# Attention projected before the convolution in two token groups, mLSTM heads taken up earlier in the weave, and first-key one-hots compared straight into fp32 rows

## The chip, the cores and the metric

The kernel runs on one core of a Trainium2 chip. The metric is the device time of one execution in microseconds (us); the median of three runs before the change is 3003.34 us (2999.98 to 3008.87). Engines are named as in the profile: PE is the tensor engine's matmul (PEld its weight load), DVE the vector engine, ACT the scalar engine, POOL the GpSimd engine, SP the engine that issues most DMAs. An engine takes its instructions in one fixed order; where the first of them waits, all behind it wait.

## The reference, cut to what matters

One decoder layer on 1024 tokens of width 1024. The normalised input is projected to an mLSTM branch (values, an output gate z, input and forget gates, and a branch that goes through a causal convolution over four tokens and a SiLU) and to an attention branch (q, k, v for 8 heads of 64). Both branches are joined, projected and added to x. Then a PEER layer picks, for each token and each of 8 heads, 16 of 16384 experts: each expert is named by a pair of keys out of 128 and 128, and the output is the gated sum of `expert_v` rows weighted by `gelu(h . expert_u)`.

```
c = silu(causal_short_conv(u) + b);  q, k = c @ wq, c @ wk        # mLSTM, per head
h = mlstm_chunkwise(q, k, v, ipre, fpre);  ym = sigmoid(z) * (rms_norm(h) + skip * c)
ya = softmax-combined dilated attention(rms_norm(qa), rms_norm(ka), va)
x = x + concat(ym, ya) @ w_out
idx, gate = top16 over (s1[key1] + s2[key2]);  a = gelu(h2 . expert_u[idx]) * gate
out = x + sum_k a[k] * expert_v[idx[k]]
```

## The kernel before, in words

Tokens are cut into eight tiles of 128 and three groups: group 0 is tiles 0 and 1, group 1 tiles 2 to 5, group 2 tiles 6 and 7. Per group the code issues `channels_in` (normalise, transpose and split the input into two fp32r parts, tiles `hth` and `htl`), `project_values` (accumulators `accvm`, `accz`), `project_gates` (`pif`, then small DVE work and transposes), `project_conv` (`accu`; then on ACT and DVE the four-tap sum `cy`, a sigmoid and a product; result `c` stored to DRAM by SP), `project_attention` (k, q, v in that order, `accqk` and `accva`; k and q normalised, transposed and stored to DRAM by ACT's queue). Every projection goes through `stream`, which loads weights `wr` in three buffers on SP's queue, rounds them on ACT (`wh`, line 170), takes the remainder on DVE (`wl`, line 172) and issues three matmuls for each product. The accumulators have two PSUM banks; for group 1 one stream fills both.

`attention` then runs over head pairs, heads and query tiles: it loads `qp`, `kp`, `vp` and the bias `bt` back from DRAM on SP, and each step computes scores (`sc`, minimum and bias on DVE, line 515, exponential on ACT) and the values of the step before. The mLSTM heads are a second generator: `weave` advances it by one half-head after every `every`-th attention step, that is after the last of each four (of each two in group 2). A half-head loads `cT`, `zs`, `vm` and two weights on SP, and is a chain of small steps over PE, ACT, DVE and POOL that ends in the product `mix` (line 476). `queries` (output projection `acco`, second norm, query projection `accq`, top 16 by DVE) follows. The four tiles of group 1 go to dense experts: their gates are spread by `spread_gates` to a table of tokens by all experts in DRAM (`gate_d`), and `dense_experts` runs all 16384 experts over these 512 tokens on PE, until the end of the program. Tiles 0, 1, 6 and 7 instead gather expert rows by indirect DMA on POOL (line 806, five buffers `gt`): steps U0, U1, V0, V1, U6, V6, U7, V7, with dot products on DVE (line 818, line 863) or, for V0 and V1, matmuls `pov` (line 849).

`spread_gates` works in groups of four tokens: DVE compares the first and the second key of each of the 128 chosen experts with the numbers 0 to 127 (line 727, two bf16 one-hot tiles `hot`), ACT copies the first to fp32 `e1` (line 731), the second is multiplied by the gate into fp32 `e2` (line 735 on ACT, four small instructions, in every other group; line 737 on DVE in the rest), four matmuls `pg` make the table's part (line 742) and ACT copies it out (line 743). There are 4 tiles x 8 blocks x 4 groups = 128 such groups. In the profile both `e1` and `e2` are called `e`.

The code gives the order of priority; a planner with its own costs places the instructions on the engines, and pulls later work (gathers, the next group's projections, queries) into holes. Tiles of a closed scope give their space to later scopes, and a tile that is placed there waits for the last reader of the old one. The scope of `hth` and `htl` is closed after the group's last projection, and for groups 1 and 2 the attention's scope is opened after that on the same side of memory.

Of the kernel before, what the change touches and what calls it, by code (L numbers as in the profile page):

```python
# [15 lines left out]
BF16 = mybir.dt.bfloat16  # L16
AF = mybir.ActivationFunctionType
ALU = mybir.AluOpType
AX = mybir.AxisListType

P = 128
# [22 lines left out]
def hybrid_layer(ctx, tc, x, g1, w_in, w_if, conv_w, conv_b, wq, wk, if_b, mh_g, skip, qn_g, kn_g,  # L44
                 rel_bias, onehot, w_out, g2, w_query, keys, expert_u, expert_ut, expert_v, out, dbg=None):
    nc = tc.nc
# [17 lines left out]
    def pool(name, side="left"):  # L64
        return tc.tile_pool(name=name, bufs=1, side=side, reuse_waits="tile")
# [32 lines left out]
    key128 = consts.tile([P, P, TQ], BF16, name="key128")  # L98
# [55 lines left out]
    def mm3(ps, lh, ll, rh, rl, first, last):  # L154
        nc.tensor.matmul(ps, lh, rh, start=first, stop=False)  # L155
        nc.tensor.matmul(ps, lh, rl, start=False, stop=False)  # L156
        nc.tensor.matmul(ps, ll, rh, start=False, stop=last)  # L157
# [8 lines left out]
    def halves(w_ap):  # L166
        wr = wts.tile([P, 512], F32, name="wr", bufs=3)
        nc.sync.dma_start(wr, w_ap)
        wh = wts.tile([P, 512], F32R, name="wh", bufs=3)
        nc.scalar.copy(wh, wr)  # L170
        wl = wts.tile([P, 512], F32R, name="wl", bufs=3)
        nc.vector.tensor_tensor(wl, wr, wh.bitcast(F32), op=ALU.subtract)  # L172
        return wh, wl
# [68 lines left out]
    def project_gates(g, cl, th, tl):  # L242
        n = GROUPS[g][1]
        W = n * P
        with pool("ga") as ga:
            pif = pst.tile([64, W], F32, name="pif", tag="tp")
            wh, wl = halves(w_if)
            for k in range(KD):
                s = slice(k * 64, (k + 1) * 64)
                mm3(pif, wh[:, s], wl[:, s], th[:, k], tl[:, k], k == 0, k == KD - 1)  # L250
            gi = ga.tile([MH, n, P], F32, name="gi")
            nc.scalar.activation(gi.rearrange("p c t -> p (c t)"), pif[0:MH], AF.Identity, bias=ifb_s[0:MH])
            gf0 = ga.tile([64, W], F32, name="gf0")
            nc.scalar.activation(gf0[32:32 + MH], pif[32:32 + MH], AF.Identity, bias=ifb_s[32:32 + MH])
            gf = ga.tile([MH, W], F32, name="gf")
            nc.vector.tensor_copy(gf, gf0[32:32 + MH])
            return gates(g, cl, ga, gi, gf)

    def project_conv(g, th, tl):

        n = GROUPS[g][1]
        W = n * P
        with pool("su") as st:
            for blk in range(2):
                accs = by_channel(stream(w_in, blk, th, tl, n, True, "u"), n)
                for h, a in enumerate(accs, 2 * blk):
                    uh = st.tile([P, 3 + W], F32, name="uh", bufs=2)
                    nc.vector.tensor_copy(uh[:, 0:3], halo[:, h])
                    nc.scalar.copy(uh[:, 3:], a)
                    nc.vector.tensor_copy(halo[:, h], uh[:, W:W + 3])  # L270
                    y = st.tile([P, W], F32, name="cy", bufs=2)
                    nc.scalar.activation(y, uh[:, 0:W], AF.Identity, scale=cw_s[:, h, 0:1], bias=cb_s[:, h:h + 1])
                    for j in range(1, 4):
                        nc.vector.scalar_tensor_tensor(y, uh[:, j:j + W], cw_s[:, h, j:j + 1], y,
                                                       op0=ALU.mult, op1=ALU.add)
                    nc.scalar.activation(uh[:, 0:W], y, AF.Sigmoid)
                    nc.vector.tensor_tensor(y, y, uh[:, 0:W], op=ALU.mult)
                    c_d[g, h] = dram.tile([P, W], F32, name=f"c{g}{h}")
                    nc.sync.dma_start(c_d[g, h], y)
# [15 lines left out]
    def by_channel(banks, n):  # L295
        return [banks[i * n // 4][:, (i * n * P) % 512:(i * n * P) % 512 + n * P] for i in range(2)]
# [11 lines left out]
    def project_attention(g, th, tl):  # L308

        tile0, n = GROUPS[g]  # L310
        with pool("sb") as st:
            for blk0, dst, gn, nm in ((8, kT_d, kg_s, "k"), (6, qT_d, qg_s, "q")):
                for blk in range(2):
                    qs = st.tile([P, n, 4, AD], F32, name="qs")
                    for b, a in enumerate(stream(w_in, blk0 + blk, th, tl, n, False, "qk")):
                        q = qs[:, 2 * b:2 * b + 2].rearrange("p c h d -> p (c h) d")
                        nc.scalar.copy(q, a.rearrange("p (h d) -> p h d", d=AD))
                        sq = st.tile([P, 8, AD], F32, name="sq")
                        nc.scalar.activation(sq, q, AF.Square)
                        ss = st.tile([P, 8], F32, name="ssq", bufs=2)  # L320
                        nc.vector.tensor_reduce(ss, sq, AX.X, ALU.add)
                        r = rstd(ss, AD, 8, st, "rq")
                        nc.vector.tensor_tensor(q, q, r[:, :, None].to_broadcast([P, 8, AD]), op=ALU.mult)
                    for pl in range(2):
                        pr = 2 * blk + pl
                        pt = pst.tile([P, n * P], F32, name="ptq", tag="tp")
                        for i in range(n):
                            nc.tensor.transpose(pt[:, i * P:(i + 1) * P], qs[:, i, 2 * pl:2 * pl + 2], ident)
                        ev = st.tile([P, n * P], F32, name="ev", bufs=2)
                        nc.scalar.activation(ev, pt, AF.Copy, scale=gn[:, pr:pr + 1])  # L330
                        dst[g, pr] = dram.tile([P, n * P], F32, name=f"{nm}T{g}{pr}")
                        nc.scalar.dma_start(dst[g, pr], ev)
            token_blocks(g, st, 10, va_d, "va", th, tl)
# [381 lines left out]
    def spread_gates(t, gb, psg):  # L715

        half = TQ
        for b in range(P // TB):
            gs = gb.tile([P, P, TB], F32, name="gs", bufs=2)
            for q in range(TB // half):  # L720
                c0 = b * TB + q * half
                ids, gate = ROWS[t]
                full = [P, P, half]
                hot = []
                for side in range(2):
                    o = gb.tile(full, BF16, name="hot", bufs=6)
                    nc.vector.tensor_tensor(o, ids[:, side, None, c0:c0 + half].to_broadcast(full),
                                            key128, op=ALU.is_equal)
                    hot.append(o.rearrange("p e t -> p t e"))
                e1 = gb.tile([P, half, P], F32, name="e1", bufs=3)  # L730
                nc.scalar.copy(e1, hot[0])
                e2 = gb.tile([P, half, P], F32, name="e2", bufs=3)
                if q % 2:
                    for j in range(half):
                        nc.scalar.activation(e2[:, j], hot[1][:, j], AF.Copy, scale=gate[:, c0 + j:c0 + j + 1])  # L735
                else:
                    nc.vector.tensor_tensor(e2, hot[1], gate[:, c0:c0 + half, None].to_broadcast([P, half, P]),
                                            op=ALU.mult)
                for j0 in range(0, half, 4):
                    pg = psg.tile([P, 4, P], F32, name="pg")  # L740
                    for j in range(4):
                        nc.tensor.matmul(pg[:, j], e1[:, j0 + j], e2[:, j0 + j], start=True, stop=True)  # L742
                    nc.scalar.copy(gs[:, :, q * half + j0:q * half + j0 + 4].rearrange("p e t -> p t e"), pg)  # L743
            nc.scalar.dma_start(gate_d[(t - GROUPS[DENSE][0]) * (P // TB) + b], gs.rearrange("p e t -> p (e t)"))
# [125 lines left out]
    def weave(main, other, every):  # L870

        for n, _ in enumerate(main):
            if n % every == every - 1:
                next(other, None)
        return other

# [5 lines left out]
    hx = channels_in(0, hs.tiles)  # L882
# [9 lines left out]
    hx = channels_in(1, hs.tiles)  # L892
# [4 lines left out]
    pt_.close()  # L897
    project_values(1, *hx)
    cols = project_gates(1, cm.tiles, *hx)
    project_conv(1, *hx)  # L900
    project_attention(1, *hx)
    hs.close()
    hs = Scope("hs2", "right")
    mx = Scope("mx1", "right")
# [7 lines left out]
    hx = channels_in(2, hs.tiles)  # L912
    project_values(2, *hx)
    cols = project_gates(2, cm.tiles, *hx)
    project_conv(2, *hx)
    project_attention(2, *hx)
    hs.close()
    drain(queries(1, ql.tiles, "left", cl.tiles, mix))
    ql2 = Scope("ql2")
# [12 lines left out]
    gb = Scope("gb", "right")  # L932
# [18 lines left out]
    for step in "U0 U1 V0 V1 U6 V6 U7 V7".split():  # L951
        t = int(step[1])
# [81 lines left out]
```

## Time and profile before

| | |
|---|---|
| median of three runs | 3003.34 us |
| profiled execution | 3002.0 us |
| its span, first to last instruction | 3000.2 us |
| mean granted TensorE clock | 0.948 of full speed |
| PE busy | 2728.0 us (91%) |
| DVE busy | 2337.4 us (78%) |
| ACT busy | 1237.2 us (41%) |
| POOL busy | 1347.6 us (45%) |
| DMA | 891.50 MB, mean 297 GB/s |

Busy time is the time in which an engine had at least one instruction under way; matmuls overlap, so a busy PE need not be at its peak. The profiled execution is 1.3 us below the median. By the trace the stages follow each other like this: group 0 to about 330 us, the projections of group 1 to about 525 us, attention and mLSTM of group 1 with projections of group 2 to about 850 us, the output and query projections of group 1 with the attention of group 2 to about 1196 us, the spread with the queries of group 2 to about 1534 us, dense experts to the end.

### The profile page before, as it was taken

Reading aid. Unit: us, or ns where it says so; the run is one execution under the profiler, and the core shown is the slowest. Engines: PE = TensorE matmul, PEld = TensorE weight load, DVE = VectorE, ACT = ScalarE, POOL = GpSimd, SP = SyncE. Lnnn points to the kernel's source line nnn. Section 1 sums busy time; section 2 is a strip of 40 time slices with the busy share of each in tenths; the row PEclk is TensorE's granted clock in tenths of the full one; section 3 lists DMA queues with packets and bytes.
Section 4 is the critical chain, followed back from the end, with each engine's and each line's share of the span. In section 5 each row is a group of like instructions: output and inputs, shape, how many; then the busy total and the mean of one; then the engine's idle time right before and its main releaser. Section 6 shows DMA issues by size and latency. Waiting matters only on the chain.

```text
span 3000.2 us, 42795 instructions
## 1 busy us (share of the span) xinstructions
PE 2728.0 (91%) x14382; PEld 2154.0 (72%) x14382; DVE 2337.4 (78%) x5522; ACT 1237.2 (41%) x2311; POOL 1347.6 (45%) x1075
## 2 busy tenths in 40 slices
PE   6978857788989999889899999999999999999999
PEld 5868657476766665567666787777788877788877
DVE  4559897678977889679843789888899888899883
ACT  4643423355534225999952233222233222233222
POOL 0100477435744445423344555555555555556540
PEclk9979978688988999999999999999999999999999
DMA  6644689788998988989898999999999999999992
GB/s 196 188 149 124 241 311 333 267 304 289 342 339 293 310 313 303 327 313 329 306 326 293 325 341 324 327 330 320 316 339 359 329 333 323 329 335 331 336 313 81
DMA packets 370897, 891.50 MB, mean 297 GB/s; under 512 B 34119, under 2 KB 135495, under 8 KB 366580
## 3 DMA queue, kind: packets, MB, share of 16 engines
q0 software_dynamic: 147456, 536.94, 50.5%
q1 hardware_dynamic: 209076, 307.78, 30.8%
q10 hardware_dynamic: 14144, 44.05, 3.8%
q8 instruction: 113, 1.85, 0.2%
q14 instruction: 108, 0.88, 0.1%
HBM read 831.97 MB, written 61.38 MB: 298 GB/s over the span
## 4 chain that ended last, share of the span: by engine, by line
PE 22%; issue 12%; POOL 8%; DMA 7%; DVE 4%; ACT 4%; POOLq 0%; DVEq 0%; ACTq 0%
POOL gt L806 8%; DMA gg<-gate_d 5%; PE pv L156 3%; PE pv L157 3%; PE pu L156 3%; PE pu L155 3%; PE pu L157 3%; PE pv L155 3%; PE pg L742 2%; ACT gs L743 1%; ACT e L735 1%; PE pov L849 1%; DMA gt<-in_expert_u_dram,idx 1%; DVE acc L863 1%; PE accq L194 1%
## 5 line engine op out<-in xcount | busy, mean ns | idle before, releaser
L806 POOL DMA_INDIRECT gt<-in_expert_u_dram,idx x512 | 661.5, 1292 | 646.7 <-DVE gt L818 428.2
L818 DVE SCALAR_TENSOR_TENSOR gt<-gt,h2s 128x1024 f32<-128x1024 f32 x512 | 617.7, 1218 | 65.5 <-DMA gt<-in_expert_u_dram,idx 64.5
L806 POOL DMA_INDIRECT gt<-in_expert_v_dram,idx x256 | 342.3, 1337 | 298.8 <-DVE acc L863 255.2
L806 POOL DMA_INDIRECT gt<-in_expert_v_dram,idxt x256 | 285.9, 1117 | 412.1 <-PE pov L849 359.5
L156 PE MATMUL pv<-vlo,dah 128*128 128x512 f32 x1024 | 402.4, 393 | 9.3 <-DVE vlo L795 9.2
L155 PE MATMUL pu<-h2th,uhi 128*128 128x512 f32 x1024 | 406.4, 397 | 0.5 <-ACT uhi L761 0.4
L156 PE MATMUL pu<-h2tl,uhi 128*128 128x512 f32 x1024 | 405.7, 396 | 0.0
L157 PE MATMUL pu<-h2th,ulo 128*128 128x512 f32 x1024 | 405.6, 396 | 0.0
L157 PE MATMUL pv<-vhi,dal 128*128 128x512 f32 x1024 | 400.4, 391 | 0.0
L793 ACT CAST vhi<-vr 128x512 fp32r<-128x512 f32 x256 | 157.5, 621 | 466.0 <-PE pv L157 459.4
L863 DVE SCALAR_TENSOR_TENSOR acc<-gt,act,acc 128x1024 f32<-128x1024 f32 x256 | 327.6, 1280 | 14.0 <-DMA gt<-in_expert_v_dram,idx 11.7
L155 PE MATMUL pv<-vhi,dah 128*128 128x512 f32 x1024 | 318.7, 394 | 8.3 <-ACT vhi L793 8.3
L170 ACT CAST wh<-wr 128x512 fp32r<-128x512 f32 x291 | 178.8, 620 | 244.9 <-DMA wr<-in_w_in_dram 50.6
L172 DVE TENSOR_TENSOR wl<-wr,wh 128x512 fp32r<-128x512 f32 x291 | 197.7, 684 | 75.4 <-ACT wh L170 72.1
L795 DVE TENSOR_TENSOR vlo<-vr,vhi 128x512 fp32r<-128x512 f32 x256 | 175.3, 686 | 89.3 <-ACT vhi L793 89.1
L156 PEld LDWEIGHTS pv<-vlo,dah 128*128 128x128 f32 x1024 | 193.0, 188 | 60.9 <-DVE vlo L795 14.9
L155 PEld LDWEIGHTS pv<-vhi,dah 128*128 128x128 f32 x1024 | 192.1, 189 | 55.9 <-ACT vhi L793 12.8
L155 PEld LDWEIGHTS pu<-h2th,uhi 128*128 128x128 f32 x1024 | 192.6, 188 | 49.8 <-ACT uhi L761 2.3
L157 PEld LDWEIGHTS pu<-h2th,ulo 128*128 128x128 f32 x1024 | 192.6, 188 | 49.8 <-issue 3.4
L156 PEld LDWEIGHTS pu<-h2tl,uhi 128*128 128x128 f32 x1024 | 192.8, 188 | 47.9 <-issue 2.5
L157 PEld LDWEIGHTS pv<-vhi,dal 128*128 128x128 f32 x1024 | 192.9, 188 | 44.0 <-issue 2.5
L761 ACT CAST uhi<-ur 128x1024 fp32r<-128x1024 f32 x128 | 134.4, 1050 | 214.9 <-PE pu L156 212.8
(278 smaller groups left out, 5596.8 us busy)
## 6 DMA issues: line engine op xcount, KB each, us to landing
ur<-in_expert_ut_dram SPq DMA_DIRECT2D x128, 512.0 KB, 6.2
vr<-in_expert_v_dram SPq DMA_DIRECT2D x256, 256.0 KB, 5.8
wr<-in_w_in_dram SPq DMA_DIRECT2D x144, 256.0 KB, 3.8
gate_d<-gs ACTq DMA_DIRECT2D x32, 1024.0 KB, 8.5
gg<-gate_d SPq DMA_DIRECT2D x16, 2048.0 KB, 20.5
wr<-in_w_query_dram SPq DMA_DIRECT2D x96, 256.0 KB, 4.7
wr<-in_w_out_dram SPq DMA_DIRECT2D x48, 256.0 KB, 4.8
gt<-in_expert_u_dram,idx POOLq DMA_INDIRECT x512, 7.0
```

The source lines that it names most:

```text
L155: nc.tensor.matmul(ps, lh, rh, start=first, stop=False)
L156: nc.tensor.matmul(ps, lh, rl, start=False, stop=False)
L157: nc.tensor.matmul(ps, ll, rh, start=False, stop=last)
L170: nc.scalar.copy(wh, wr)
L172: nc.vector.tensor_tensor(wl, wr, wh.bitcast(F32), op=ALU.subtract)
L742: nc.tensor.matmul(pg[:, j], e1[:, j0 + j], e2[:, j0 + j], start=True, stop=True)
L761: nc.scalar.copy(uh, ur)
L793: nc.scalar.copy(vh, vr)
L795: nc.vector.tensor_tensor(vl, vr, vh.bitcast(F32), op=ALU.subtract)
L806: nc.gpsimd.indirect_dma_start(out=gt, out_offset=None, in_=table, in_offset=bass.IndirectOffsetOnAxis(ap=idx[:, j:j + 1], axis=0))
L818: nc.vector.scalar_tensor_tensor(gt, gt, 1.0, h2, op0=ALU.mult, op1=ALU.mult, accum_out=pr[:, j:j + 1])
L863: nc.vector.scalar_tensor_tensor(acc, gt, COEF[t][:, j:j + 1], acc, op0=ALU.mult, op1=ALU.add)
```

## The change

Three edits. `spread_gates` compares the first keys directly into the fp32 tile `e1`, with tokens outside and keys inside, so the first `hot` tile and the ACT copy are gone; `hot` has three buffers in place of six. `weave` advances the mLSTM after the first attention step of each stretch of `every`, not after the last. In groups 1 and 2 `project_attention` is issued before `project_conv`; group 0 keeps its order.

```
                 e1 = gb.tile([P, half, P], F32, name="e1", bufs=3)
-                nc.scalar.copy(e1, hot[0])
+                nc.vector.tensor_tensor(e1, ids[:, 0, c0:c0 + half, None].to_broadcast([P, half, P]),
+                                        key128.rearrange("p e t -> p t e"), op=ALU.is_equal)
+                o = gb.tile(full, BF16, name="hot", bufs=3)
+                nc.vector.tensor_tensor(o, ids[:, 1, None, c0:c0 + half].to_broadcast(full), key128,
+                                        op=ALU.is_equal)
+                hot = o.rearrange("p e t -> p t e")
...
         for n, _ in enumerate(main):
-            if n % every == every - 1:
+            if n % every == 0:
                 next(other, None)
...
     cols = project_gates(1, cm.tiles, *hx)
+    project_attention(1, *hx)
     project_conv(1, *hx)
-    project_attention(1, *hx)
...
     cols = project_gates(2, cm.tiles, *hx)
+    project_attention(2, *hx)
     project_conv(2, *hx)
-    project_attention(2, *hx)
```

## Rows read from the trace of the kernel before

**Rows 1.** The page's head: span, and busy time by engine.
```profile
span 3000.2 us, 42795 instructions
PE 2728.0 (91%) x14382; PEld 2154.0 (72%) x14382; DVE 2337.4 (78%) x5522; ACT 1237.2 (41%) x2311; POOL 1347.6 (45%) x1075
```

**Rows 2.** Windows: stretch, length, busy PE PEld DVE ACT POOL, clock, DMA, GB/s.
```profile
419.00:432.00 13.00, 0.00 (x0) 0.00 (x0) 13.00 (x23) 2.34 (x4) 8.44 (x7) 0.62 0.93 326
...
834.00:848.00 14.00, 1.32 (x8) 0.73 (x6) 11.83 (x30) 1.78 (x7) 8.88 (x8) 0.67 1.05 405
...
1196.00:1320.00 124.00, 99.73 (x728) 74.92 (x720) 84.16 (x200) 112.40 (x232) 47.41 (x41) 0.92 0.89 320
1320.00:1500.00 180.00, 157.57 (x1213) 124.86 (x1207) 159.26 (x708) 175.40 (x347) 62.34 (x54) 0.98 0.88 317
1500.00:1534.00 34.00, 29.33 (x166) 19.48 (x165) 24.37 (x51) 26.95 (x43) 20.26 (x13) 0.90 0.88 306
1534.00:2924.00 1390.00, 1372.25 (x5962) 1090.53 (x5961) 1124.99 (x1513) 405.13 (x611) 727.23 (x549) 1.00 0.94 329
2924.00:3000.00 76.00, 69.09 (x302) 56.33 (x300) 27.38 (x40) 17.13 (x27) 0.00 (x0) 0.97 0.24 83
```

**Rows 3.** Longest waits of PE from 400 to 560: total us, times, longest.
```profile
PE accqk L194 <- ACT qs L317: 16.0, 3, 13.3
PE sc L513 <- DMA kp<-kT: 14.8, 1, 14.8
PE sc L513 <- DVE mx L515: 5.5, 1, 5.5
```

**Rows 4.** Timeline, group 1's convolution end: start, us, engine, line, idle before it.
```profile
404.78 0.58 ACT L269 COPY uh<-accu 128x512 f32<-128x512 f32 x1 [2.67 <-PE accu L194]
...
431.54 1.07 ACT L317 COPY qs<-accqk 128x512 f32<-128x512 f32 x2 [3.95 <-DVE cy L277]
```

**Rows 5.** Timeline of PE's last value projection and SP's first attention load.
```profile
524.46 0.28 PE L194 MATMUL accva<-wh,htl 128*128 128x256 f32 x1
...
524.54 0.42 SPq L486 DMA_DIRECT2D qp<-qT  x1
```

**Rows 6.** SP's own waits, 330 to 960.
```profile
SPq L168 <- DVE wl L172: 286.4, 75, 22.4
...
SPq L279 <- DVE cy L277: 11.2, 5, 3.8
```

**Rows 7.** Timeline, last mLSTM half-head of group 1 behind its attention.
```profile
822.98 0.66 PE L547 MATMUL pty<-ident,ya 128*128 128x128 f32 x4 [1.06 <-DVE ya L543]
...
844.10 0.69 PE L472 MATMUL pth<-ident,hn 128*128 128x128 f32 x2 [9.69 <-DVE hn L469]
```

**Rows 8.** Groups by line, 1196 to 1540: count, busy, mean ns, idle before.
```profile
L743 ACT COPY gs<-pg 128x512 f32<-128x512 f32 x128 | 130.5, 1061 | 13.5 <-PE pg L742 13.3
...
L727 DVE TENSOR_TENSOR hot<-ids,key 128x512 bf16<-128x512 bf16 x256 | 101.8, 418 | 32.3 <-ACT e L731 25.3 <-ACT e L735 5.8
L735 ACT ACTIVATE e<-hot,grow 128x128 f32<-128x128 bf16 x256 | 84.8, 414 | 0.0
L731 ACT CAST e<-hot 128x512 f32<-128x512 bf16 x128 | 84.5, 670 | 2.7 <-PE pg L742 2.6
...
L737 DVE TENSOR_TENSOR e<-hot,grow 128x512 f32<-128x512 bf16 x64 | 43.6, 683 | 12.8 <-PE pg L742 12.6
```

**Rows 9.** The convolution's tap line: ns least, median, most; both sizes together.
```profile
L274 DVE SCALAR_TENSOR_TENSOR cy<-uh,cw_s,cy x36: 464/480/750, 52.4 to 733.1; 128x256 f32<-128x256 f32 x24, 128x512 f32<-128x512 f32 x12
```

**Rows 10.** Windows of the gathers' line alone (POOL busy, count).
```profile
327.00:960.00 633.00, 324.92 (x261) 0.84 0.89 312
...
1196.00:1534.00 338.00, 128.82 (x106) 0.95 0.88 317
```

**Rows 11.** Window of the `pov` matmuls inside the dense stage.
```profile
1534.00:1670.00 136.00, 22.37 (x168) 3.30 (x168) 0.68 (x1) 1.00 0.89 308
```

**Rows 12.** Timeline of DVE, the last gathered row's work.
```profile
2923.37 1.27 DVE L863 SCALAR_TENSOR_TENSOR acc<-gt,act,acc 128x1024 f32<-128x1024 f32 x1
```

More of the change, by code (lines that the diff above doesn't have):

```diff
@@ L723, in spread_gates @@
                 full = [P, P, half]
[L724 to L729, printed above, removed]
-                e1 = gb.tile([P, half, P], F32, name="e1", bufs=3)
-                nc.scalar.copy(e1, hot[0])
+                e1 = gb.tile([P, half, P], F32, name="e1", bufs=3)
+                nc.vector.tensor_tensor(e1, ids[:, 0, c0:c0 + half, None].to_broadcast([P, half, P]),
[4 more added lines that the diff above has]
+                hot = o.rearrange("p e t -> p t e")
                 e2 = gb.tile([P, half, P], F32, name="e2", bufs=3)
@@ L734, in spread_gates @@
                     for j in range(half):
-                        nc.scalar.activation(e2[:, j], hot[1][:, j], AF.Copy, scale=gate[:, c0 + j:c0 + j + 1])
+                        nc.scalar.activation(e2[:, j], hot[:, j], AF.Copy, scale=gate[:, c0 + j:c0 + j + 1])
                 else:
-                    nc.vector.tensor_tensor(e2, hot[1], gate[:, c0:c0 + half, None].to_broadcast([P, half, P]),
+                    nc.vector.tensor_tensor(e2, hot, gate[:, c0:c0 + half, None].to_broadcast([P, half, P]),
                                             op=ALU.mult)
```

## The prediction

> **What bounds the kernel now.** I read the page's head, then windows by stage, then waits and timelines where PE is empty. The head has PE busy for 91% of the span and DVE for 78% [rows 1]. The last stage, dense experts from 1534, has PE busy for 1372 of 1390 us and again for 69 of the last 76, in which POOL does nothing [rows 2]; PE sets that stage, and the change doesn't touch its work. What the change can move is how early this stage begins. Before it the limits differ.
>
> In the spread (1196 to 1534, 338 us; the three windows of rows 2) ACT is busy for 112.4 + 175.4 + 27.0 = 314.8 us, 93%, DVE for 84.2 + 159.3 + 24.4 = 267.8 (79%) and PE for 99.7 + 157.6 + 29.3 = 286.6 (85%) [rows 2]. ACT paces it: DVE waits 25.3 us for ACT's copy of `e` and PE's pieces follow [rows 8].
>
> In group 1 PE has three empty places. From 419 to 432 it does nothing [rows 2]: the next k projection needs a PSUM bank which ACT's copy `qs` is to empty, and that copy stands in ACT's order behind the convolution's chain, which runs from the accumulator's copy at 405 to the DVE product that lets `qs` go at 431.5; the longest wait is 13.3 us [rows 3, 4]. At 524.5 the last value projection ends and SP loads `qp` 0.08 us later [rows 5]; scores wait 14.8 us for `kp`, then 5.5 for DVE [rows 3]. From 834 to 848 PE is busy for 1.3 of 14 us at a clock of 0.67 [rows 2]: attention's last transposes are at 823, but the last mLSTM half-head, issued after the last attention step, reaches its own transposes at 844 after a 9.7 us wait for DVE [rows 7], and the output projection needs it.
>
> **The change, part by part.** All sums are against the profiled execution's 3002.0 us (span 3000.2 and 1.8 around it); the median of the runs is 1.3 above it, which is added at the end.
>
> *First keys into fp32.* Gone are 128 ACT copies, 84.5 us busy [rows 8], so ACT has 230.3 us left in the stage. Of the 256 bf16 compares at 418 ns, 128 become compares with an fp32 output and a key operand that strides. The trace has no such compare. Its nearest row is line 737: the same two layouts read, the same 128x512 fp32 written, 683 ns; that is the value taken. Ends: 418 (the bf16 compare) [rows 8] and 750 (the slowest three-operand fp32 instruction of that size) [rows 9]; a lower price than 418 is excluded, since neither elements nor written bytes shrink. At 683 DVE gains 128 x 0.265 = 33.9 us and stands at 301.7, more than ACT's 230.3 and PE's 286.6. So DVE becomes the engine that ends last, and the gain is not the 84.5 us removed. I take it that DVE gets as full as ACT is now, 93%, since its largest waits, 25.3 and 5.8 us for ACT, go with the copy: 301.7 / 0.93 = 324, a gain of 14 us. Packed to 100%: 301.7, gain 36. At DVE's present 79%: 382, a loss of 44. At 750 ns DVE has 310.3 and the stage 334, gain 4. At 418 ns PE is next: 286.6 / 0.93 = 308, gain 30. Three `hot` buffers for one tile per group instead of six for two are the same depth: nothing.
>
> The Trainium skill, page "VectorE: DVE Perf Modes", section "The perf-mode tier table", says that a two-tensor operation runs at double rate only where everything is 16-bit, and at single rate with fp32. It speaks against this change: by it the fp32 output alone costs the compare its double rate, and the sum is the one above; without it the 30 us of the lower end would stand. No row here shows the compare itself.
>
> *Attention before the convolution, group 1.* Its 24 weight loads on SP now come ahead of the convolution's 8 and its 4 `c` stores; SP's queue is paced by the weight buffers' release (286.4 us of waits for `wl`, 75 times), not by the `c` stores (11.2 us) [rows 6], so the order costs nothing there by itself. The 13.3 us hole goes, because `qs` no longer stands behind the convolution's chain [rows 3, 4]. What is late next: `qp` was loaded right behind the last reader of the input tiles [rows 5]. I read that as the wait for their space, which now ends with the convolution's last matmul. Then the 14.8 us for `kp` stay, and attention's first minimum on DVE meets the convolution's last chain, which took 26 us from the accumulator's copy [rows 4]. Most of that chain lies in the wait for `kp`; I give back 5 us, about the wait for DVE there now [rows 3]. Net 8 us. Ends: 28 (the hole goes and the convolution also covers the 14.8) and a loss of 13 (13.3 gained, a chain of 26 us wholly in front of the scores). Group 2's swap lies in attention of group 1, beside which its projections run; nothing, and up to 5 either way.
>
> *mLSTM ahead.* Its waits are added where a half-head now stands earlier: its `cT` load waits for the `c` store, behind it on SP stand `zs`, `vm`, weights and the next `kp`; on PE its first matmul holds the scores behind it. Heads 0 and 1 come from the convolution's first block, so I take no cost. The last half-head of group 1 now has three attention steps behind it, so the 9.7 us of rows 7 and the rest of 834 to 848 (14.0 - 1.3 = 12.7 us empty) lie beside those steps: 13 us. Ends: 0 (DVE, 11.8 of 14 us busy there [rows 2], merely shifts its queue) and 20 (from attention's end, 823, to 844, less what matmuls of the half-head still cost). Groups 0 and 2: nothing taken.
>
> *Given back.* POOL issued 261 gathers in 633 us before 960, one per 2.43 us, and 106 in the spread, one per 3.19 [rows 10]. The 21 us of group 1 and 14 of the spread leave 9 + 4 = 13 gathers to later, which end as `pov` matmuls inside the dense stage, where PE has no room: 42 gathers cost it 22.4 us there, 0.53 each [rows 11]. 7 us.
>
> **Sum:** 3002.0 - 14 - 8 - 13 + 7 = 2974; with 1.3 to the median, 2975. The gathers' last work on DVE is at 2923 [rows 12] and holds its place, as the dense stage starts earlier and has more of them; PE's end near 2972 is still behind it.
>
> **The rivals.**
> 1. The spread does not shorten: DVE's order, filled with the top 16 of group 2 and 159 of 180 us busy from 1320 [rows 2], takes up what ACT gives. 3002 - 21 + 9 x 0.53 = 2986, median 2987. For it: that window. Against: from 1196 DVE has 40 of 124 us free.
> 2. The reorder doesn't do what it says: the planner, which places work by its own costs, puts the convolution or the half-heads where they were. 3002 - 14 + 2 = 2990, median 2991. For it: group 2's projections already lie far from their place in the code. Against: the hole at 419 and the tail at 844 follow the code's order.
> 3. All goes well: spread packed (36), group 1's hole and the `kp` wait both covered (28), tail 13, 28 gathers later x 0.53 = 15 back: 2940, median 2941. For it: DVE's waits for ACT were the larger part of its idle time [rows 8]. Against: space of the input tiles.
> 4. Slower: the longer compare leads DVE's order, and DVE keeps its present 79% fill because its remaining waits (PE's `pg`, weights, gather pairs) stay in the same proportion. The spread takes 382 us, +44; 3002 + 44 - 21 - 2 (four gathers fewer later) = 3023, median 3024. It decides once DVE's fill falls under some 85%, where the stage is 355 and eats group 1's gain. For it: the queue is in order, and DVE is in front of both PE and ACT in each group of four. Against: its biggest named waits are the ones removed.
>
> **How the numbers follow.** Chances: forecast 0.44, rival 1 0.17, rival 2 0.14, rival 3 0.10, rival 4 0.15. What a measurement of this kernel can tell from no change is about 0.3%, 9 us. Faster by more (under 2994): nearly all of the forecast, 0.41, most of rival 1, 0.14, over half of rival 2, 0.08, rival 3 0.10: 0.73. Slower (over 3012): rival 4, 0.14. Within: 0.13. The range leaves out half of rival 3 below and most of rival 4 above: 2944 to 3010. The forecast's own is 2958 to 2990.
>
> **What would show it.** In the changed profile: no 128x512 ACT copy to `e`, and 128 compares of 128x512 fp32 near 683 ns on DVE; from the first to the last `pg` some 324 us, with DVE fuller than ACT. PE's wait for `qs` of 13 us gone, and a wait for `kp` of some 15 us still in front of the first scores, now behind `accu` and not `accva`. The last `pth` of group 1 ahead of attention's last `pty`, and no empty 14 us between. More than 42 gathers' `pov` in the dense stage, whose own length stays. Wrong it would be if the spread stays over 335 us (rivals 1, 4), if a first mLSTM half-head holds PE for its `c` load, or if the gathers end after the dense matmuls.

## The result and the profile after

The changed kernel takes 2975.64 us (median of four runs, 2968.47 to 2979.17) where before stands at 3006.11 (four runs, 2999.98 to 3011.11): 0.9886 of it, 95% interval 0.9863 to 0.9909. The quotient of two medians can differ a little from the ratio given (here it is 0.9899); it lies within the interval here and in all comparisons below. The profiled execution took 2979.17 us, 22.8 less than that of before. The forecast of 2975 came out; several of its terms did not.

The head of the page after, to be read beside [rows 1]:

```profile
span 2977.3 us, 42658 instructions
PE 2728.4 (92%) x14382; PEld 2147.5 (72%) x14382; DVE 2365.6 (79%) x5520; ACT 1180.9 (40%) x2187; POOL 1353.4 (45%) x1075
```

PE's busy time is the same (2728.0 before). What the change bought is 23 us less of empty PE.

The windows of the kernel after, columns as in [rows 2]: the old hole behind the convolution, the mLSTM's tail, the spread in three parts, the dense stage and its end:

```profile
405.00:432.00 27.00, 19.05 (x136) 17.53 (x136) 21.89 (x41) 8.99 (x16) 20.98 (x16) 0.94 0.95 330
800.00:818.00 18.00, 0.88 (x7) 0.72 (x7) 10.93 (x24) 0.96 (x5) 9.92 (x11) 0.56 0.99 363
1174.00:1280.00 106.00, 94.58 (x718) 73.88 (x717) 87.16 (x196) 83.97 (x175) 51.68 (x35) 0.95 0.91 333
1280.00:1460.00 180.00, 157.62 (x1241) 121.59 (x1239) 178.45 (x704) 147.83 (x287) 80.12 (x63) 0.99 0.94 342
1460.00:1475.00 15.00, 12.18 (x73) 8.75 (x74) 14.12 (x33) 10.68 (x17) 13.78 (x5) 1.00 0.77 278
1475.00:2901.00 1426.00, 1398.97 (x6084) 1101.73 (x6083) 1123.55 (x1527) 413.20 (x616) 721.41 (x569) 0.99 0.94 327
2901.00:2977.00 76.00, 69.22 (x303) 56.41 (x301) 40.84 (x53) 17.16 (x27) 10.24 (x7) 0.97 0.42 146
```

Three readings. The hole at 419 is gone. The empty place in front of the last mLSTM transposes is not: it has moved to 800 and is longer, PE busy for 0.88 of 18 us at a clock of 0.56. The spread is DVE's now: 178.45 of 180 us in its middle, where ACT has 147.83.

PE's longest waits from 400 to 560 after, as [rows 3] (who waits, for whom, us in total, times, longest; chosen lines):

```profile
PE sc L513 <- DMA kp<-kT: 8.8, 1, 8.8
PE accva L194 <- ACT ev L305: 7.0, 1, 7.0
PE sc L513 <- DVE mx L515: 5.8, 1, 5.8
PE accqk L194 <- ACT qs L317: 3.0, 2, 1.5
```

`qs` holds PE for 1.5 us at most where it was 13.3, `kp` for 8.8 where it was 14.8, and DVE's first minimum for 5.8 where it was 5.5. The last projection of group 1 ends at 503.5 (524.5 before) and the first scores stand at 512.7 (539.6).

The spread's groups after, from 1174 to 1475, as [rows 8] (chosen lines):

```profile
L742 ACT COPY gs<-pg 128x512 f32<-128x512 f32 x127 | 129.9, 1057 | 34.5 <-PE pg L741 27.6 <-issue 4.8 <-DMA gate_d<-gs 1.5
...
L725 DVE TENSOR_TENSOR e<-ids,key 128x512 f32<-128x512 bf16 x125 | 85.1, 685 | 7.4 <-PE pg L741 5.8 <-PE accq L194 1.4 <-issue 0.2
...
L728 DVE TENSOR_TENSOR hot<-ids,key 128x512 bf16<-128x512 bf16 x125 | 50.9, 419 | 3.0 <-issue 2.2 <-ACT e L734 0.7
```

The new compare takes 685 ns (683 forecast), and the waits of 25.3 and 5.8 us for ACT [rows 8] are gone but for 0.7.

### The profile page after: what moved, and what is told of

The parts are those of the page before. It is cut to its first block, busy times and chain, and to the rows that moved or that the text cites. A ratio compares the mean times of both kernels' runs of the same rounds, so it can differ in the third digit from the quotient of the medians.

```text
span 2977.3 us, 42658 instructions
## 1 busy us (share of the span) xinstructions
PE 2728.4 (92%) x14382; PEld 2147.5 (72%) x14382; DVE 2365.6 (79%) x5520; ACT 1180.9 (40%) x2187; POOL 1353.4 (45%) x1075
## 4 chain that ended last, share of the span: by engine, by line
PE 57%; DMA 16%; DVE 13%; issue 7%; POOL 3%; ACT 2%; SPq 0%; DVEq 0%; ACTq 0%; POOLq 0%
DMA gg<-gate_d 7%; PE pu L156 6%; PE pu L157 6%; PE pu L155 6%; PE pv L156 5%; PE pv L157 5%; PE pv L155 5%; DMA gt<-in_expert_v_dram,idxt 3%; PE accq L194 3%; POOL gt L805 3%; PE acco L194 3%; PE pov L848 2%; PE sc L513 2%; PE po L535 2%; DVE gt L817 2%
## 5 line engine op out<-in xcount | busy, mean ns | idle before, releaser
L805 POOL DMA_INDIRECT gt<-in_expert_u_dram,idx x512 | 650.9, 1271 | 692.3 <-DVE gt L817 441.4
L817 DVE SCALAR_TENSOR_TENSOR gt<-gt,h2s 128x1024 f32<-128x1024 f32 x512 | 618.1, 1219 | 58.0 <-DMA gt<-in_expert_u_dram,idx 55.1
L805 POOL DMA_INDIRECT gt<-in_expert_v_dram,idxt x256 | 308.9, 1207 | 373.6 <-PE pov L848 307.7
L156 PEld LDWEIGHTS pv<-vlo,dah 128*128 128x128 f32 x1024 | 193.4, 189 | 59.0 <-DVE vlo L794 10.6
```

Source lines behind the costliest of these rows:

```text
L805: nc.gpsimd.indirect_dma_start(out=gt, out_offset=None, in_=table, in_offset=bass.IndirectOffsetOnAxis(ap=idx[:, j:j + 1], axis=0))
L817: nc.vector.scalar_tensor_tensor(gt, gt, 1.0, h2, op0=ALU.mult, op1=ALU.mult, accum_out=pr[:, j:j + 1])
```

## The experiments

All ran beside the kernel before on their chip, whose median was 3009.57, 3008.13 and 3006.88 us in the three sets. The table holds what the trace of each gives: the first scores of group 1, the first and last `pg` of the spread (us), and, counted from the windows of the dense stage's matmuls `pu` and `pv`, how many of the 6144 were left at 1700 us and how many PE did from 1700 to 2900. How much earlier than before a kernel reaches a point is called its head start; what it loses of that later it gives back. A trace is one execution; its time lies up to 19 us from the median of its kernel, so a sum over a trace is held against the span of that trace.

| kernel | ratio to before, 95% | first `sc` | first, last `pg` | left at 1700 | done to 2900 | span |
|---|---|---|---|---|---|---|
| before | | 539.6 | 1203.0, 1533.0 | 5490 | 5083 | 3000.2 |
| whole change | 0.9886 (0.9863-0.9909) | 512.7 | 1174.9, 1474.8 | 5369 | 5062 | 2977.3 |
| e1 spread alone | 0.9992 (0.9974-1.0011) | 540.8 | 1213.5, 1514.6 | 5466 | 5070 | 2997.8 |
| e2 order alone | 0.9876 (0.9833-0.9919) | 511.8 | 1158.4, 1487.7 | 5368 | 5056 | 2978.3 |
| e3 weave alone | 1.0051 (1.0029-1.0073) | 540.5 | 1231.8, 1572.9 | 5636 | 5123 | 3025.5 |
| e4 order, weave | 0.9941 (0.9912-0.9971) | 508.6 | 1161.7, 1501.6 | 5391 | 5066 | 2981.4 |
| f1 order, spread | 0.9897 (0.9867-0.9927) | 508.4 | 1169.0, 1472.7 | 5396 | 5075 | 2980.4 |
| f2 order, group 1 | 0.9996 (0.9971-1.0020) | 514.6 | 1159.9, 1481.1 | 5412 | 5031 | 2994.4 |
| f3 order, group 2 | 1.0027 (1.0001-1.0053) | 544.4 | 1217.9, 1547.4 | 5603 | 5093 | 3029.1 |
| f4 all, weave in group 1 only | 0.9923 (0.9895-0.9951) | 512.3 | 1158.3, 1455.0 | 5318 | 5064 | 2965.2 |
| h1 before, no U6 V6 U7 V7 | 0.9893 (0.9867-0.9919) | 537.1 | 1200.7, 1549.5 | 5462 | 5202 | 2966.3 |
| h2 f2, no U6 V6 U7 V7 | 0.9758 (0.9732-0.9785) | 506.9 | 1146.8, 1487.9 | 5260 | 5203 | 2919.7 |
| h3 whole, no U6 V6 U7 V7 | 0.9780 (0.9754-0.9806) | 510.0 | 1163.6, 1460.6 | 5299 | 5201 | 2929.0 |

### The three edits apart: e1 to e4

e1, against before:

```
-                hot = []
-                ...
-                nc.scalar.copy(e1, hot[0])
+                nc.vector.tensor_tensor(e1, ids[:, 0, c0:c0 + half, None].to_broadcast([P, half, P]),
+                                        key128.rearrange("p e t -> p t e"), op=ALU.is_equal)
...
```

> The kernel before with the spread edit alone (first keys compared straight into fp32 rows). My sum: 14 us off the spread, 2 given back as gathers' matmuls in the dense stage, so 12 us under the kernel before, and the group 1 milestones (first scores at 540, last mLSTM transposes at 844) where they were. Rival, from the changed kernel's trace, in which the spread is 30 us shorter: 30 off the spread, but 10 to 20 of it back in the dense stage. Rival that the vector engine's order takes it all up: no change within 9 us.

3006.54 us, 0.9992: nothing, although first to last `pg` fell from 330 to 301 us. The number is that of the last forecast, the spread's 29 us that of the second; none of them lasts to the end.

e2, against before, in groups 1 and 2:

```
+    project_attention(1, *hx)
     project_conv(1, *hx)
-    project_attention(1, *hx)
```

> The kernel before with attention's projection ahead of the convolution in groups 1 and 2, nothing else. My sum: the 13.3 us hole at 419 goes, 5 come back at the first scores, 8 us at the first scores and about 4 in the whole. Rival, from the changed kernel's trace, where the first scores come 27 us earlier: 20 to 27 us at the first scores with this edit alone, and 10 to 20 us in the whole, if nothing behind it takes them back.

2978.08 us, 0.9876: as much as the whole change, and more than either forecast. The first scores come 27.8 us earlier. The last `pth` of group 1 lies 31 us behind the last `pty` (21 before) after a wait of 22.6 us for `hn`, though the weave is the old one.

e3, against before:

```
-            if n % every == every - 1:
+            if n % every == 0:
```

> The kernel before with the mLSTM advanced after the first attention step of each stretch, nothing else. My sum: the last mLSTM transposes of group 1 ahead of attention's last transposes, the empty 13 us at 834 gone, about 10 us under the kernel before. Rival, from the changed kernel's trace, in which the last mLSTM transposes come 43 us behind attention's last ones: the mLSTM is a chain of its own that ends when it ends; the last half-head stays behind attention, the empty place stays and the whole moves by less than 6 us.

3027.88 us, 1.0051: a loss of 18 us against its base. The first matmul of an mLSTM head in group 1 did not come earlier (551.1, before 551.6), the attention stage, from first scores to last `pty`, took 294.6 us instead of 283.8, and the last `pth` came at 857 instead of 844, 22 us behind the last `pty` as it was 21 before. Neither forecast had the loss; the rival had the place of the last half-head.

e4 is e2 and e3 together.

> The kernel before with both reorders, without the spread edit. My sum: 21 us off at the start of the output projection, 16 in the whole. Rival, that the group 1 part is a 27 us gain of the order alone and the mLSTM tail takes a part of it back: output projection's end 25 us earlier as in the changed kernel, 15 to 25 in the whole; and with the spread alone the two add up to the whole change's 30 us, or to more if the dense stage takes both back.

2997.12 us, 0.9941: the weave costs beside the new order too, though the two intervals touch (0.9912 against e2's 0.9919); between e4 and the whole change (0.9886) stands the spread edit alone. So the gain is the order's, the weave is no gain, and the spread's 30 us show in the total only behind the other two, if at all. The last set asks for the order without the weave.

### Which group's order, which weave: f1 to f4

f1 is e1 and e2 together, f2 and f3 are e2 in one group only.

> The order in both groups and the spread edit, the weave as before. If the three edits simply add, this is the order's gain (0.9876 of before) and the spread's (0.9992): 0.987, some 2970 us where before stands at 3009. If the spread pays more where the stage begins earlier, as it did behind order and weave together (0.9886 against 0.9941, 0.55%), this is 0.982, some 2956 us, and faster than the whole change. If the whole change owes its time to the weave after all, this stays at or above 0.9886. The spread stage should last 300 us in either case, and first scores should stand at 512.

2979.15 us, 0.9897. Neither faster than the whole change nor than e2: the three intervals overlap over most of their width. The edits don't add. No version tried beats the whole change measurably.

> The order swapped in group 1 alone. Theory 1, that of the prediction: the gain lies in group 1's own projections (hole at 419 gone, first scores 28 us earlier at 512), and group 2's swap is worth nothing; then at least 22 of the 31 us are here, ratio 0.990 or less. Theory 2: group 2's swap shortens the attention of group 1, beside which its projections run (284 us before, 261 with both swaps); then first scores stand at 512, attention still takes 284, and the ratio is 0.995 or more.

> The order swapped in group 2 alone. Theory 1: first scores at 540 as before and a ratio between 0.997 and 1.003. Theory 2: first scores at 540, attention of group 1 in 261 us instead of 284, and a ratio of 0.995 or less.

f2 3003.04 us (0.9996), f3 3016.49 (1.0027). Both theories fail: each swap by itself gives nothing or a small loss, and the two together 1.2%. Theory 2 had the ratio of f2, but not its attention: from first scores to last `pty` this takes 273.6 us in f2 and 272.1 in f3, 261.1 in e2, where before has 283.8. So each swap shortens it by 10 to 12 us, which the prediction had at nothing for group 2. The trace shows where f2's gain goes. Up to the last `pg` it is as early as e2 (1481 against 1488), so all that I had said of group 1 is there; yet it ends 16 us later. The dense stage gives it back. The head start is 52 us at the last `pg`. At 1700 it is 78 matmuls fewer left, which is 18.4 us at the 236 ns that a dense matmul takes there (in before: 1293 us from 1700 to PE's end at 2993, over 5490), and in the next 1200 us PE does 52 fewer than before, another 12.3: 6 remain, and the spans differ by 5.8. Of the 33.5 us gone by 1700, 11.5 are `pov` matmuls (256 behind the last `pg`, before 168), 11.4 an empty PE and 3.9 dense matmuls that no longer run ahead of the last `pg`; the rest isn't accounted for, with the clock there at 0.97 instead of 0.99.

f4, against the whole change:

```
-    def weave(main, other, every):
+    def weave(main, other, every, first=0):
...
-            if n % every == 0:
+            if n % every == first:
...
-    drain(weave(attention(0, mx.tiles, mix), mlstm_half(0, 0, mx.tiles, cols, mix), 4))
+    drain(weave(attention(0, mx.tiles, mix), mlstm_half(0, 0, mx.tiles, cols, mix), 4, 3))
...
-    drain(weave(attention(2, mx.tiles, mix), mlstm_half(2, 0, mx.tiles, cols, mix), 2))
+    drain(weave(attention(2, mx.tiles, mix), mlstm_half(2, 0, mx.tiles, cols, mix), 2, 1))
```

> The whole change, but the mLSTM is taken up earlier in group 1 alone; groups 0 and 2 keep the old place. Theory 1: the weave costs through group 1, where the last half-head still ends 43 us behind the last attention transpose; then the time is that of the whole change, 0.9886. Theory 2: the weave costs in groups 0 and 2 (in group 2 every second step); then this is faster than the whole change by 10 us or more, 0.985 or less.

2985.62 us, 0.9923: the second theory falls, since 0.985 lies outside the interval; the first's 0.9886 lies just outside too. With f1 beside it (0.9897 without the weave, 0.9886 with it), whether and where the weave costs when the spread edit is present is below what these runs tell.

### What gives a head start back: h1 to h3

h1, against before; h2 and h3 the same line in f2 and in the whole change:

```
-    for step in "U0 U1 V0 V1 U6 V6 U7 V7".split():
+    for step in "U0 U1 V0 V1".split():
```

> The kernel before without the steps U6, V6, U7 and V7 (512 gathers and their dot products; the rows of tiles 6 and 7 are not put out). It is the base for the next two: in the full kernels the last 512 gathers run beside the dense stage from 1650 to some 2910 us. Theory 1, that these gathers give a head start back through waits in the dense stage: PE's waits there (25 us empty, 17.5 of them for the experts' rounded weights) go and the clock stays full, some 2975 us. Theory 2, that the dense stage's length is PE's own work: within 10 us of before. The spread still begins near 1203 and ends near 1533.

> The order swapped in group 1 alone, without U6, V6, U7 and V7. With all gathers the last matmul of the spread came 52 us earlier (1533 to 1481) and the end 5. Theory 1: without the later gathers the head start stays, less the matmuls of V0 and V1 that move into the dense stage (11.5) and some 5 us of dense matmuls no longer done early: 35 us below the same kernel without the swap. Theory 2: the give-back is in PE's work and is there without these gathers too: 10 us below or less.

> The whole change without U6, V6, U7 and V7. The spread's last matmul came 58 us earlier and the end 23. Theory 1: 58 less 13 for V0 and V1 and 5 for dense matmuls, 40 us below the kernel before without these steps. Theory 2: 25 us below, as with all gathers.

Medians 2973.58, 2929.32 and 2941.99 us. h1 is where its theory 1 had it, 33 us under before. h2 lies 44.3 us under h1, where the same swap was worth nothing with all gathers: theory 1 (35), well clear of theory 2 (10 or less). h3 lies 31.6 under h1, between the two forecasts of 40 and 25, and tells less.

From 1700 to 2900 us, the windows of f2 and then of h2 (same columns):

```profile
1700.00:2900.00 1200.00, 1175.33 (x5033) 950.60 (x5032) 1014.78 (x1356) 350.09 (x528) 649.16 (x482) 0.99 0.94 326
```

```profile
1700.00:2900.00 1200.00, 1200.00 (x5205) 976.97 (x5204) 481.83 (x649) 365.68 (x541) 0.00 (x0) 1.00 0.38 117
```

Without the gathers PE is never empty, its clock is full, and all three kernels do 5201 to 5203 dense matmuls in these 1200 us: what is ahead at 1700 stays ahead to the end (h2: 202 matmuls by 231 ns = 46.7 us, spans 46.6; h3: 163, 37.7, spans 37.3). With the gathers the DMA engines are 0.94 busy, DVE 85%, and PE is empty for 25 us of f2's window. f2's waits on PE in its dense stage are, against 9.2 and 8.3 us for the first two in before:

```profile
PE pv L156 <- DVE vlo L795: 14.8, 10, 3.9
PE pv L155 <- ACT vhi L793: 13.5, 9, 5.6
PE pv L155 <- ACT dah L151: 5.3, 1, 5.3
PE pov L849 <- DMA gt<-in_expert_v_dram,idxt: 1.6, 1, 1.6
```

That the gathers take what is lost behind 1700 is shown by h1 and h2. For the larger part, up to 1700, it is shown in part only: f2 loses 33.5 of 51.9 us there, and h2 still loses 15 of 61.6. And without these steps the planner also starts dense matmuls earlier beside the spread (first `pu` at 1442 in h1 and 1503 in before, 1414 in h2 and 1467 in f2; h1's last `pg` comes at 1549.5, where 1533 was expected), so part of the 47 us at 1700 is its new order. Whether DVE's turn or DMA was late for each rounded weight wasn't separated.

### What holds the last mLSTM half-head: h4

```
-    for step in "U0 U1 V0 V1 U6 V6 U7 V7".split():
+    for step in "U6 V6 U7 V7".split():
```

> The whole change without the steps U0, U1, V0 and V1 (their rows are not put out), so that no gather's dot product stands on DVE while group 1's mLSTM runs. Read for the distance from attention's last transposes (pty) to the last mLSTM half-head's (pth): 43 us in the whole change. Theory 1: the chain of a half-head is stretched by dot products that wait for their gathers, one between each two of its small DVE steps; then the distance falls to 20 us or less, and the wait for hn from 17 to under 6. Theory 2: the half-heads are late by their own place, behind the attention steps and group 2's projections; then it stays over 35 us.

One execution, whose time is of no use here. The last transposes of group 1, by tile (count: shortest/median/longest ns, first and last start):

```profile
L472 PE MATMUL pth<-ident,hn x2: 272/300/328, 679.4 to 679.6; 128*128 128x128 f32 x2
...
L547 PE MATMUL pty<-ident,ya x4: 421/421/476, 702.3 to 703.0; 128*128 128x128 f32 x4
```

The last half-head is 23 us ahead of attention's last transposes instead of 43 behind. The eight half-heads follow each other every 25.8 us (498.8 to 679.4, in seven steps) instead of every 36.4 (563.5 to 818.1), and from 480 to 960 PE has no wait for `hn` of 0.5 us or more. Both of theory 1's signs are there, none of theory 2's. The whole change shows the mechanism in its timeline, in the last half-head (chosen lines: the half-head's own steps, and between them the dot products L817 that wait for a gather):

```profile
803.76 0.15 DVE L462 SCALAR_TENSOR_TENSOR sm<-num 128x2 f32<-128x2 f32 x1
804.18 1.23 DVE L817 SCALAR_TENSOR_TENSOR gt<-gt,h2s 128x1024 f32<-128x1024 f32 x1 [0.26 <-DMA gt<-in_expert_u_dram,idx]
805.33 0.16 DVE L463 TENSOR_TENSOR sm<-sm,ecol 128x2 f32<-128x2 f32 x1
808.63 1.23 DVE L817 SCALAR_TENSOR_TENSOR gt<-gt,h2s 128x1024 f32<-128x1024 f32 x1 [3.15 <-DMA gt<-in_expert_u_dram,idx]
809.78 0.16 DVE L465 SCALAR_TENSOR_TENSOR sm<-sm 128x2 f32<-128x2 f32 x1
811.15 1.23 DVE L817 SCALAR_TENSOR_TENSOR gt<-gt,h2s 128x1024 f32<-128x1024 f32 x1 [1.21 <-DMA gt<-in_expert_u_dram,idx]
812.30 0.16 DVE L466 SCALAR_TENSOR_TENSOR sm<-sm 128x2 f32<-128x2 f32 x1
813.62 0.73 POOL L467 TENSOR_TENSOR sm<-sm,mhalf 128x2 f32<-128x2 f32 x1
813.70 1.23 DVE L817 SCALAR_TENSOR_TENSOR gt<-gt,h2s 128x1024 f32<-128x1024 f32 x1 [1.24 <-DMA gt<-in_expert_u_dram,idx]
816.11 1.23 DVE L817 SCALAR_TENSOR_TENSOR gt<-gt,h2s 128x1024 f32<-128x1024 f32 x1 [1.18 <-DMA gt<-in_expert_u_dram,idx]
817.26 0.42 DVE L469 TENSOR_TENSOR hn<-num,sm 128x256 f32<-128x256 f32 x1
817.83 0.66 PE L472 MATMUL pth<-ident,hn 128*128 128x128 f32 x2 [17.12 <-DVE hn L469]
```

Five steps from L462 to L467 have 0.15 + 3 x 0.16 + 0.73 = 1.36 us of work and take from 803.76 to `hn` at 817.26, 13.5 us, because a dot product that waits for its gather stands behind each of the DVE steps, and two in front of `hn`. The waits of these five for their gathers are 7.0 of the 13.5 us, their own work from start to start is 5.8. Which of the two stretches the chain more isn't separated by h4, since it takes out both: from 460 to 680 us its DMA engines are 0.44 busy and DVE for 119 of 220 us, in the whole change from 512 to 775 0.87 and 212 of 263.

## Why the prediction came out, step by step

**First keys into fp32: mechanism right, size 14 where the trace has 30.** DVE is the bound, the compare is 685 ns, and DVE is 93% full from first to last `pg` (278.6 of 299.9 us), the fill that I took. The windows, before and then after (columns as in [rows 2]):

```profile
1203.00:1533.30 330.30, 279.52 (x2047) 214.69 (x2044) 260.79 (x941) 308.20 (x608) 125.15 (x103) 0.95 0.89 318
```

```profile
1174.90:1474.80 299.90, 263.28 (x2020) 203.12 (x2019) 278.63 (x928) 242.48 (x478) 144.56 (x100) 0.98 0.92 336
```

What failed is the 301.7 us of DVE work. It was read from 1196 to 1534, 8 us more than from first to last `pg`; there DVE had 260.8 us, which with the 33.9 of the compares makes 294.7. And I held all other DVE work of the stage in place, but 16 us of that is no longer inside. None of the 30 us reaches the end by itself: in e1, 10.5 us are lost before the first `pg`, about half of it where PE's waits for the gathers of V0 and V1 (`pov`) rise from 6.7 to 12.0 us between 1112 and the spread, and the rest in the dense stage. The spread edit puts off the first `pg` beside the other edits too (f1 behind e2 by 10.6 us, the whole change behind e4 by 13.2).

**Attention before the convolution, group 1: the hole right, size 8 where first scores came 27 earlier.** The 13.3 us went as forecast. `kp` is still waited for, 8.8 us where it was 14.8. The reading of [rows 5] as a wait for the space of the input tiles doesn't hold: SP's own order is enough, and its loads go out before the last reader of these tiles is through. Before and then after:

```profile
524.16 0.33 SPq L168 DMA_DIRECT2D wr<-in_w_in_dram  x1
524.54 0.42 SPq L486 DMA_DIRECT2D qp<-qT  x1
```

```profile
500.03 0.33 SPq L168 DMA_DIRECT2D wr<-in_w_in_dram  x1
500.40 0.42 SPq L486 DMA_DIRECT2D qp<-qT  x1
503.58 0.33 SPq L279 DMA_DIRECT2D c<-cy  x1
503.96 0.42 SPq L489 DMA_DIRECT2D kp<-kT  x1
```

In both, `qp` follows a weight load at once. After, it goes out 3.1 us before the convolution's last matmul, which starts at 503.54, and `kp` stands behind a store of `c` that waited 2.7 us for `cy`; in h4 `kp` goes out at 458.80, before that matmul (459.10). The 5 us for a meeting of the convolution's chain with the first scores were not lost (5.8 us for DVE, 5.5 before). Waits of the q transposes for `qs` and `ev` fell from 10.2 to 6.1 us, and from 330 to the last projection PE's own busy time fell from 141.8 to 137.4 us, at a granted clock of 0.91 where it was 0.85; neither was in the sum. "Group 2's swap: nothing" failed: it shortens attention of group 1, and with it the gain of group 1 lasts, without it it doesn't (e2, f2).

**mLSTM ahead: failed.** Forecast were 13 us, from "three attention steps behind it". The last `pth` lies 43 us behind the last `pty` after, 21 before, and the wait for `hn` is 17.1 us where it was 9.7 [rows 7]; the order alone makes it 31 (e2). The half-heads are paced by their own chains on DVE, not by the step after which they are issued: from first `pq` to last `pth` before has 293 us, the weave alone 306, the whole change 290, h4 209. h4 shows what stretches them. The lower end of 0 that I had named, "DVE merely shifts its queue", was the nearest.

**Given back: 7 us forecast, 35 found.** The forecast's "whose own length stays" failed: from the last `pg` to the end of the span before has 1466.9 us, the whole change 1502.2. The windows up to 1700, before and then after, and the `pov` matmuls after:

```profile
1533.30:1700.00 166.70, 166.61 (x777) 116.25 (x777) 80.76 (x131) 45.83 (x69) 73.68 (x60) 0.99 0.91 319
```

```profile
1475.10:1700.00 224.90, 217.94 (x1017) 146.39 (x1016) 103.94 (x172) 59.89 (x85) 88.79 (x85) 0.98 0.93 322
```

```profile
1475.10:2977.30 1502.20, 35.53 (x264) 5.22 (x264) 1.37 (x2) 0.99 0.92 318
```

The head start at the last `pg` is 58.2 us. At 1700 it is 121 matmuls, 28.6 us: gone are 13.2 for `pov` (264 in the dense stage, 35.53 us, against 168 and 22.37 [rows 11]), 6.9 for a PE that is empty for 7.0 us between the last `pg` and 1700 (0.1 before), 5.8 for dense matmuls that no longer run ahead of the last `pg`, and 3.7 left over, with the clock there at 0.98 instead of 0.99. To 2900 another 21 matmuls are lost, 5.0 us. 58.2 - 29.6 - 5.0 = 23.6; the spans differ by 22.9. The forecast had the `pov` price of 0.53 us right and counted 13 gathers where 24 to 25 moved (13.2 by 0.53); waits and early dense matmuls it did not have. That the gathers' last work on DVE would hold its place at 2923 was right (2923.4 after).

**Sum.** 35 us of head start less 7 was forecast; 58 less 35 came. Head start and give-back were both too small, by 23 and 28 us. So the total was right by errors that cancel, which is luck, and of the rivals the third had the nearer picture of group 1 and the spread. The fourth is excluded by the spread of 300 us, the second by the hole, though the late last half-head that it also allowed for stayed; the first by the same 300 us, though in e1 its result, no gain, is what the spread edit came to.

## What to carry to other kernels

Where a last stage is full on PE and shares DMA and DVE with a stream of gathers, a head start is not a gain until the work that it meets there is counted: count what is left at a fixed time in that stage, and what is done per stretch after it. A chain of short steps on an engine that also takes long instructions which wait for DMA is as slow as what stands between its steps; here issuing it earlier in the code did not make it end earlier (e3), and taking the other work out of its gaps did (h4). Edits that are each worth nothing can be worth 1.2% together, so parts of a change are not to be added up from single trials.

## What was not expected

A single execution of one kernel moves with the mean granted clock: the order alone ran from 2949.06 us at 0.954 to 2992.03 at 0.945 within one set. Why both swaps are needed stays open: up to the last `pg` f2 and e2 are alike (1481 and 1488 us), and in the dense stage f2 has PE empty for 43.5 us against 33.1 and does 25 matmuls fewer from 1700 to 2900; which of the planner's orders there causes it was not tried.
